# Other costs for TensorE's products and a longer table of places in a list scheduler: the same 5635 instructions in another order

## The chip, the cores and the metric

The kernel runs on one core of a Trainium2 chip. The metric is the device time of one execution in microseconds (us). Five engines work side by side, each through its own instructions in a fixed order: TensorE (PE, products and transposes; its weight loads are listed as PEld), VectorE (DVE), ScalarE (ACT), GpSimd (POOL) and SyncE (SP, which issues most transfers). An instruction also waits for semaphores that other engines raise.

## The reference

```python
def hybrid_parallel_heads_encoder(x, ...):          # x: 1 x 256 x 1024, fp32, two layers
    ...
    h = rms_norm(x, norm1_g) @ w_in                 # 1024 -> 2560: q, k, v of three groups
    a = neighbourhood_attention(...)                # 4 heads
    d = dilated_window_attention(...)               # 6 heads
    c = grouped_query_attention(...)                # 6 heads, 2 of k and v
    x = x + rms_norm of each group, joined @ w_out
    g, u = split(rms_norm(x, norm2_g) @ w_gate_up)  # 1024 -> 2 x 2816
    g = depthwise convolution of width 3 over g, + bias
    x = x + (silu(g) * u) @ w_down                  # 2816 -> 1024
```

## The kernel before

Every fp32 product is made as three products of two parts, `hi` (the value cut to the product format) and `lo` (what is left): hi*hi, lo*hi and hi*lo. So each weight chunk that lands in a `wp_raw` buffer is cast to `wp_hi` on ACT, and DVE subtracts the two into `wp_lo`. The sequence is two tiles of 128 tokens. A layer has an attention part (projections from `act_hT`, the normalised and transposed input; scores, softmax, transposes of the probabilities, products with the values; the output projection from `act_mixT`) and a feed-forward part in 11 steps of 256 columns, each with a gate (G), an up (U) and a down product. Products collect in PSUM tiles `psa_a` (four buffers) and `psw_w` (four buffers).

Nothing of this is issued as it is written. Each call only adds an operation to a list (class `Plan`); `order()` then plays through a list scheduler in which each operation has a cost from `cost()`, each handover between engines one from `HANDOVER`, and each buffer a time from which it is free. Of all operations that are ready it takes the one that can start earliest; where several can, the one with the lowest rank decides. The rank is the operation's number in the list plus a shift; `PLACES` adds to the rank of single operations, by their number. `emit()` (line 472) issues everything in that order, so every instruction of the trace carries that line. The order on each engine is fixed when the program is built; on the chip the engines only wait for each other.

Names that the prediction uses: `const_x` is the residual, and holds the result at the end; `act_s2k` is scratch; `act_z` and `act_sw` serve the rotary embedding; `act_nab` is the neighbourhood bias, which POOL copies out of `small_few`; `small_ms`, `small_rstd` and `small_rx` are statistics of the norms; `act_ch` and `act_cl` are the hi and lo part of one step's activation in the feed-forward part. The very last product tile of layer 2 is cut in two halves of 256 columns, so that its second half, `end`, has a PSUM tile of its own, a DVE instruction of 256 columns and an output transfer of 128 KB.

Of the kernel before, what the change touches and what calls it, by code (L numbers as in the profile page):

```python
# [224 lines left out]
def handover(a, b):  # L225
# [1 line left out]


PLACES = {
# [6 lines left out]
}  # L236


class Plan:
# [30 lines left out]
    def add(self, engine, method, args, kw):  # L270
# [14 lines left out]
        if method == "matmul" and not kw["start"]:  # L285
            ins.append(args[0])
        o.ns, o.lat, o.size, o.kind = cost(engine.name, method, args, kw, ins)
        func = args[2] if method == "activation" else None
        if func in (AF.Exp, AF.Gelu) and func != self.table:
# [185 lines left out]
def cost(engine, method, args, kw, ins):  # L475

    out = args[0]
    if method == "dma_start":
        w = out if isinstance(out, View) else args[1]
        small = min(out.shape[-1], args[1].shape[-1]) < 128  # L480
        spread = isinstance(args[1], bass.AP) and args[1].ap[0][0] == 0
        stored = isinstance(out, View) and out.tile.pool.dram
        size = 4 * math.prod(w.shape) * (2 if small or spread else 1.5 if stored else 1)
        return 620 if engine == "POOL" else 480, 0, size, None
    n = out.width()
    psum = any(v.tile.pool.psum for v in ins)
    if engine == "PE":
        if method == "transpose":
            return n / 2.25 + 2.5, 0, 0, "turn"
        n = args[2].width()  # L490
        ns = {512: 231.6, 384: 174.5, 256: 118.0}.get(n, n / 2.25 + 2.5)
        if args[1].dtype == mybir.dt.bfloat16:
            ns = 213.0
        return ns, 0, 0, "half" if args[1].shape[0] < P else "full"
    if engine == "ACT":
        extra = 88 * sum(isinstance(kw.get(k), View) for k in ("scale", "bias")) + 92 * ("accum_out" in kw)
        ns = 0.833 * n + (53 if psum else 95) + extra
        return ns, ns + (15 if "accum_out" in kw else 105), 0, None
    if engine == "DVE":
        if method in ("reduce_sum", "reduce_max"):  # L500
            n = args[1].width()
        ns = 1.04 * n + (126 if method == "scalar_tensor_tensor" else 68)
        return ns, ns + 82, 0, None
    if method == "memset":
        ns = 190 + 0.83 * n
    elif method == "tensor_copy":
        ns = 0.92 * n + 100
    elif kw.get("op") == ALU.pow:
        ns = 560 + 150 * n
    elif method == "tensor_scalar":  # L510
        ns = 350 + 3.8 * n
    else:
        ns = 830 if out.width() == S else 350 + 3.1 * n
    return ns, ns - 95, 0, None
# [1046 lines left out]
```

## Time and profile before

| | |
|---|---|
| time, median of 3 runs | 604.28 us (603.97 to 604.68) |
| the profiled execution's own time | 604.39 us |
| its span in the trace | 602.6 us |
| PE busy | 596.9 us |
| DVE, ACT, POOL busy | 484.9, 428.5, 81.0 us |

The span runs from the first instruction to the last; 1.8 us of the profiled execution's time lie around it. Where the engine that is busy nearly all the time stands still, the whole kernel gets longer; where another engine does, that costs nothing by itself.

### The profile page before, as it was taken

The numbers are of one execution on the slowest core, as the hardware profiler recorded it, in microseconds if no ns is written. First come the engines' busy times: TensorE is split into PE (matmuls) and PEld (weight loads), VectorE is DVE, ScalarE is ACT, GpSimd is POOL, SyncE is SP. The second block draws the span as 40 slices with busy tenths as digits, with TensorE's granted clock in tenths as the row PEclk, the third lists the DMA queues.
The fourth block names the chain that finished last, engine by engine and source line by source line (L and its number), as shares of the span: only waits on it lengthen the run. The fifth ranks groups of instructions, "written<-read, shape, count | busy, mean of one in ns | idle before, by whom it ended". The sixth has DMA issues, their size and how long they took to land.

```text
span 602.6 us, 9916 instructions
## 1 busy us (share of the span) xinstructions
PE 596.9 (99%) x3496; PEld 524.7 (87%) x3496; DVE 484.9 (80%) x995; ACT 428.5 (71%) x1065; POOL 81.0 (13%) x130
## 2 busy tenths in 40 slices
PE   8999999999999999999999999999999999999997
PEld 7999898888888888888899989888888888888886
DVE  4899988997788988888777898777977777777775
ACT  6889999686566767666688899676766556666661
POOL 2733030102400000000023213421000000000000
PEclk9999999999999999999999999999999999999999
DMA  8893313557588898999444726844465556555501
GB/s 281 294 329 114 106 36 108 196 188 238 174 243 292 274 358 310 327 308 298 155 143 159 258 71 245 281 177 140 140 210 202 171 188 210 173 179 208 194 16 70
DMA packets 85218, 121.44 MB, mean 202 GB/s; under 512 B 9881, under 2 KB 69881, under 8 KB 85169
## 3 DMA queue, kind: packets, MB, share of 16 engines
q1 hardware_dynamic: 82896, 112.17, 55.8%
q0 software_dynamic: 1728, 8.39, 4.1%
q8 instruction: 27, 0.44, 0.3%
q10 hardware_dynamic: 544, 0.26, 0.1%
q14 instruction: 23, 0.18, 0.1%
HBM read 110.93 MB, written 9.88 MB: 200 GB/s over the span
## 4 chain that ended last, share of the span: by engine, by line
PE 97%; ACT 1%; DVE 1%; POOL 0%; issue 0%; DVEq 0%; POOLq 0%
PE psw_w L472 53%; PE psa_a L472 44%; ACT act_s2k L472 0%; POOL small_rstd L472 0%; ACT act_z L472 0%; DVE act_z L472 0%; ACT act_hT L472 0%; DVE wp_lo L472 0%; DVE act_sw L472 0%; POOL small_ms L472 0%; DVE const_x L472 0%; DVE act_qo L472 0%; ACT wp_hi L472 0%; POOL const_warm L472 0%; DVEq L472 0%
## 5 line engine op out<-in xcount | busy, mean ns | idle before, releaser
L472 DVE TENSOR_TENSOR wp_lo<-wp_raw,wp_hi 128x512 fp32r<-128x512 f32 (+2 forms) x332 | 231.8, 733 | 57.1 <-ACT wp_hi L472 41.1
L472 ACT CAST wp_hi<-wp_raw 128x512 fp32r<-128x512 f32 (+2 forms) x332 | 203.0, 663 | 21.7 <-PE psw_w L472 10.1
L472 PE MATMUL psw_w<-act_hT,wp_hi 128*128 128x512 f32 x704 | 180.3, 393 | 0.0
L472 PEld LDWEIGHTS psw_w<-act_hT,wp_hi 128*128 128x128 f32 x704 | 127.3, 188 | 24.5 <-DVE act_hT L472 0.6
L472 PE MATMUL psa_a<-wp_hi,act_hT 128*128 128x384 f32 (+2 forms) x448 | 112.6, 331 | 0.7 <-ACT wp_hi L472 0.7
L472 PEld LDWEIGHTS psw_w<-act_hT,wp_lo 128*128 128x128 f32 x704 | 97.2, 188 | 7.1
L472 PE MATMUL psw_w<-act_hT,wp_lo 128*128 128x256 f32 x704 | 101.3, 280 | 0.0
L472 PEld LDWEIGHTS psa_a<-wp_hi,act_hT 128*128 128x128 f32 x448 | 78.2, 188 | 3.4 <-ACT wp_hi L472 0.9
L472 PE MATMUL psa_a<-wp_lo,act_hT 128*128 128x384 f32 (+2 forms) x224 | 74.2, 333 | 0.1
L472 ACT COPY act_s2k<-psw_w 128x256 f32<-128x256 f32 x88 | 32.3, 372 | 58.5 <-PE psw_w L472 58.1
L472 PE MATMUL psa_a<-wp_lo,act_ch 128*128 128x512 f32 (+1 forms) x176 | 68.2, 387 | 0.0
L472 PE MATMUL psa_a<-wp_hi,act_ch 128*128 128x512 f32 x176 | 68.1, 388 | 0.0
L472 PE MATMUL psa_a<-wp_hi,act_cl 128*128 128x512 f32 (+1 forms) x176 | 67.6, 388 | 0.0
L472 DVE TENSOR_TENSOR act_s2k<-psw_w,act_s2k 128x256 f32<-128x256 f32 x88 | 36.7, 422 | 12.2 <-ACT act_s2k L472 11.8
L472 PEld LDWEIGHTS psa_a<-wp_lo,act_hT 128*128 128x128 f32 x224 | 42.1, 188 | 2.3 <-DVE wp_lo L472 1.0
L472 PEld LDWEIGHTS psa_a<-wp_hi,act_cl 128*128 128x128 f32 x176 | 33.1, 188 | 6.8
L472 PEld LDWEIGHTS psa_a<-wp_hi,act_ch 128*128 128x128 f32 x176 | 33.0, 188 | 6.2
L472 PEld LDWEIGHTS psa_a<-wp_lo,act_ch 128*128 128x128 f32 x176 | 33.1, 188 | 6.0
L472 DVE SCALAR_TENSOR_TENSOR act_s2k<-act_s2k,act_cw,act_s2k 128x255 f32<-128x255 f32 x88 | 36.8, 478 | 1.4 <-ACT act_s2k L472 1.3
L472 ACT ACTIVATE act_s2k<-act_s2k 128x512 f32<-128x512 f32 x22 | 13.9, 632 | 30.2 <-DVE act_s2k L472 30.2
L472 ACT ACTIVATE act_s2k<-act_s2k,act_cw 128x256 f32<-128x256 f32 x44 | 24.1, 595 | 15.4 <-DVE act_s2k L472 15.4
L472 POOL TENSOR_TENSOR small_rstd<-small_ms,const_mh 128x6 f32<-128x6 f32 (+2 forms) x26 | 30.8, 1186 | 14.2 <-DVE small_ms L472 12.6
(132 smaller groups left out, 791.7 us busy)
## 6 DMA issues: line engine op xcount, KB each, us to landing
wp_raw<-in_w_gate_up_dram SPq DMA_DIRECT2D x44, 1024.0 KB, 5.0
wp_raw<-in_w_down_dram SPq DMA_DIRECT2D x22, 1024.0 KB, 7.3
wp_raw<-in_w_in_dram SPq DMA_DIRECT2D x14, 768.0 KB, 5.9
wp_raw<-in_w_in_dram SPq DMA_DIRECT2D x8, 1024.0 KB, 7.0
wp_raw<-in_w_out_dram SPq DMA_DIRECT2D x8, 768.0 KB, 7.8
dram_khi<-act_mixT_hi SPq DMA_DIRECT2D x4, 768.0 KB, 3.6
dram_klo<-act_mixT_lo SPq DMA_DIRECT2D x4, 768.0 KB, 8.4
wp_lo<-dram_klo POOLq DMA_DIRECT2D x4, 768.0 KB, 5.0
```

The source lines that it names most:

```text
L472: getattr(o.engine.real, o.method)(*map(real, o.args), **{k: real(v) for k, v in o.kw.items()})
```

## The change

Three numbers in `cost()` are new, the times that the scheduler counts for a product of 512, 384 and 256 columns, and the table `PLACES` goes from 50 to 126 entries. No operation is added, removed or altered: what changes is where each stands on its engine.

```diff
 PLACES = {
-    375: -35, 488: 15, 528: -53, 550: 173, 587: -78, 594: 125, 616: -286, 646: -9, 709: -79, 750: -226, 752: -396,
+    71: -45, 87: 313, 90: -10, 97: 334, 125: 1139, 202: 544, 261: 285, 305: 481, 340: 437, 347: 207, 356: 412,
...
         n = args[2].width()
-        ns = {512: 231.6, 384: 174.5, 256: 118.0}.get(n, n / 2.25 + 2.5)
+        ns = {512: 228.6, 384: 173.8, 256: 117.8}.get(n, n / 2.25 + 2.5)
```

The orders differ most in the two attention parts and little in the feed-forward parts. Three places follow. The number behind a name is the buffer's and the tile's; a tile's can differ between the two programs by a little.

First, ACT at the start, some 13 us in: `wp_hi1` is cast from the second weight buffer, and `act_s2k...small_ssx` are squares of the residual, which the norm's statistics need. Before:

```order
L472 ACTIVATE act_hT0_146<-psw_w3_166,const_gains0_122 128x256
L472 ACTIVATE act_hT0_146<-psw_w1_117,const_gains0_122 128x256 x2
L472 ACTIVATE act_s2k4_223,small_ssx0_163<-const_x0_79 128x512
L472 ACTIVATE act_hT0_146<-psw_w2_124,const_gains0_122 128x256 x2
L472 ACTIVATE act_s2k0_81,small_ssx0_163<-const_x0_79 128x512
L472 CAST wp_hi1_240<-wp_raw1_138 128x384 x4
L472 CAST wp_hi0_141<-wp_raw2_153 128x384 x4
```

and after the change:

```order
L479 ACTIVATE act_s2k3_202,small_ssx0_163<-const_x0_79 128x512
L479 ACTIVATE act_hT0_146<-psw_w1_117,const_gains0_122 128x256 x2
L479 ACTIVATE act_s2k4_221,small_ssx0_163<-const_x0_79 128x512
L479 ACTIVATE act_hT0_146<-psw_w2_124,const_gains0_122 128x256
L479 CAST wp_hi1_233<-wp_raw1_138 128x384 x3
L479 ACTIVATE act_hT0_146<-psw_w2_124,const_gains0_122 128x256
L479 CAST wp_hi1_233<-wp_raw1_138 128x384
L479 ACTIVATE act_s2k0_81,small_ssx0_163<-const_x0_79 128x512
L479 CAST wp_hi0_141<-wp_raw2_153 128x384 x4
```

The last square stood ahead of the four casts from `wp_raw1`; it now stands behind them, and three of the casts also go ahead of the last `act_hT`.

Second, PE in the first projections, some 25 us in: the products into `psa_a3` are the keys of the dilated group for the second token tile, those into `psa_a0` are its values for the first, from the weights `wp_hi0` and `wp_lo0`. Before:

```order
L472 MATMUL psa_a3_332<-wp_hi1_240,act_hT0_146 128x384 x2
L472 MATMUL psa_a3_332<-wp_lo1_248,act_hT0_146 128x384
L472 MATMUL psa_a3_332<-wp_hi1_240,act_hT0_146 128x384 x2
L472 MATMUL psa_a3_332<-wp_lo1_248,act_hT0_146 128x384
L472 MATMUL psa_a3_332<-wp_hi1_240,act_hT0_146 128x384
L472 MATMUL psa_a0_157<-wp_hi0_141,act_hT0_146 128x384
L472 MATMUL psa_a0_157<-wp_lo0_149,act_hT0_146 128x384
L472 MATMUL psa_a0_157<-wp_hi0_141,act_hT0_146 128x384 x2
L472 MATMUL psa_a0_157<-wp_lo0_149,act_hT0_146 128x384
L472 MATMUL psa_a0_157<-wp_hi0_141,act_hT0_146 128x384 x2
L472 MATMUL psa_a0_157<-wp_lo0_149,act_hT0_146 128x384
L472 MATMUL psa_a0_157<-wp_hi0_141,act_hT0_146 128x384
```

and after the change:

```order
L479 MATMUL psa_a3_331<-wp_lo1_240,act_hT0_146 128x384
L479 MATMUL psa_a3_331<-wp_hi1_233,act_hT0_146 128x384
L479 MATMUL psa_a0_157<-wp_hi0_141,act_hT0_146 128x384
L479 MATMUL psa_a0_157<-wp_lo0_149,act_hT0_146 128x384
L479 MATMUL psa_a0_157<-wp_hi0_141,act_hT0_146 128x384 x2
L479 MATMUL psa_a0_157<-wp_lo0_149,act_hT0_146 128x384
L479 MATMUL psa_a0_157<-wp_hi0_141,act_hT0_146 128x384 x2
L479 MATMUL psa_a0_157<-wp_lo0_149,act_hT0_146 128x384
...
L479 MATMUL psa_a3_331<-wp_hi1_233,act_hT0_146 128x384
L479 MATMUL psa_a3_331<-wp_lo1_240,act_hT0_146 128x384
L479 MATMUL psa_a3_331<-wp_hi1_233,act_hT0_146 128x384 x2
L479 MATMUL psa_a3_331<-wp_lo1_240,act_hT0_146 128x384
```

The last six products of the keys now come after the values' first tile and a part of their second, so the values' first product stands six products earlier on PE.

Third, PE at the very end: `psw_w1` (before: `psw_w0`) is the half tile `end`. Before:

```order
L472 MATMUL psw_w0_83<-wp_lo1_248,act_ch1_828 128x256
L472 MATMUL psw_w0_83<-wp_hi1_240,act_cl1_838 128x256
L472 MATMUL psa_a0_157<-wp_lo0_149,act_ch0_762 128x512
L472 MATMUL psa_a0_157<-wp_hi0_141,act_cl0_783 128x512
L472 MATMUL psa_a0_157<-wp_hi1_240,act_ch1_828 128x512
L472 MATMUL psa_a0_157<-wp_lo1_248,act_ch1_828 128x512
L472 MATMUL psa_a0_157<-wp_hi1_240,act_cl1_838 128x512
L472 MATMUL psa_a0_157<-wp_hi1_240,act_ch1_828 128x512
L472 MATMUL psa_a0_157<-wp_lo1_248,act_ch1_828 128x512
L472 MATMUL psa_a0_157<-wp_hi1_240,act_cl1_838 128x512
```

and after the change:

```order
L479 MATMUL psw_w1_117<-wp_hi0_141,act_cl0_783 128x256
L479 MATMUL psw_w1_117<-wp_hi0_141,act_ch0_762 128x256
L479 MATMUL psw_w1_117<-wp_lo0_149,act_ch0_762 128x256
L479 MATMUL psw_w1_117<-wp_hi0_141,act_cl0_783 128x256
L479 MATMUL psw_w1_117<-wp_hi1_233,act_ch1_833 128x256
L479 MATMUL psw_w1_117<-wp_lo1_240,act_ch1_833 128x256
L479 MATMUL psw_w1_117<-wp_hi1_233,act_cl1_842 128x256
L479 MATMUL psw_w1_117<-wp_hi1_233,act_ch1_833 128x256
L479 MATMUL psw_w1_117<-wp_lo1_240,act_ch1_833 128x256
L479 MATMUL psw_w1_117<-wp_hi1_233,act_cl1_842 128x256
```

Before, the last products were eight of 512 columns into a whole tile; now they are those of the half tile, 256 columns each. The same holds behind them: DVE's last instruction and the last output transfer are now those of the half tile.

## Rows read from the trace of the kernel before

**Rows 1.** The page: busy time of PE with its share and instructions; TensorE's granted clock.

```profile
PE 596.9 (99%) x3496; PEld 524.7 (87%) x3496; DVE 484.9 (80%) x995; ACT 428.5 (71%) x1065; POOL 81.0 (13%) x130
...
PEclk9999999999999999999999999999999999999999
```

**Rows 2.** Windows, the start: stretch, length, then busy time of each engine.

```profile
0.00:16.00 16.00, 14.34 (x79) 11.52 (x80) 7.70 (x18) 10.99 (x27) 4.42 (x14) 1.00 0.88 287
```

**Rows 3.** The chain that ended last, one feed-forward step: start, length, what.

```profile
438.30 11.12 PE psw_w L472 x64
449.42 5.45 PE psa_a L472 x24
```

**Rows 4.** Timeline at the start, ACT and PE: start, us, instruction, idle before.

```profile
12.98 0.64 ACT L472 ACTIVATE act_s2k<-const_x 128x512 f32<-128x512 f32 x1
...
13.59 0.93 ACT L472 CAST wp_hi<-wp_raw 128x384 fp32r<-128x384 f32 x2
...
14.16 0.62 PE L472 MATMUL psa_a<-wp_hi,act_hT 128*128 128x384 f32 x2 [0.67 <-ACT wp_hi L472]
```

**Rows 5.** Timeline 24 to 29 us, and one row at 33 us; POOL, DVE, PE.

```profile
24.11 2.16 POOL L472 COPY act_nab<-small_few 28x1984 f32<-28x1984 f32 x1
...
24.49 1.96 DVE L472 TENSOR_TENSOR act_sw<-act_z,small_sdq 128x48 f32<-128x48 f32 x2
26.37 0.55 DVE L472 TENSOR_TENSOR wp_lo<-wp_raw,wp_hi 128x384 fp32r<-128x384 f32 x1
...
27.31 0.55 DVE L472 TENSOR_TENSOR wp_lo<-wp_raw,wp_hi 128x384 fp32r<-128x384 f32 x1
...
27.70 0.33 PE L472 MATMUL psa_a<-wp_lo,act_hT 128*128 128x384 f32 x1
...
28.21 0.33 PE L472 MATMUL psa_a<-wp_lo,act_hT 128*128 128x384 f32 x1
...
32.98 0.68 DVE L472 TENSOR_TENSOR act_sw<-act_z,small_sdk 128x48 f32<-128x48 f32 x2
```

**Rows 6.** Timeline of PE at 34 us.

```profile
34.42 0.34 PE L472 MATMUL psa_a<-wp_hi,act_hT 128*128 128x384 f32 x1
34.84 0.44 PE L472 MATMUL psa_a<-wp_lo,act_hT 128*128 128x384 f32 x1
```

**Rows 7.** Timeline 94 to 97 us, DVE and PE: first score tile, transposes.

```profile
94.70 0.42 DVE L472 CUSTOM_DVE_ANT_0 act_s2k<-psw_w,act_nab 128x256 f32<-128x256 f32 x1 [0.26 <-PE psw_w L472]
...
96.08 0.69 DVE L472 TENSOR_TENSOR wp_lo<-wp_raw,wp_hi 128x512 fp32r<-128x512 f32 x1
...
95.87 0.60 PE L472 MATMUL psw_w<-const_ident,act_s2k 128*128 128x128 f32 x4
```

**Rows 8.** Timeline of PE where layer 1's attention ends.

```profile
119.39 0.39 PE L472 MATMUL psa_a<-wp_hi,act_mixT_lo 128*128 128x512 f32 x1
119.78 0.50 PE L472 MATMUL psw_w<-act_hT,wp_hi 128*128 128x512 f32 x1
120.11 0.28 PE L472 MATMUL psw_w<-act_hT,wp_lo 128*128 128x256 f32 x1
```

**Rows 9.** The end: timeline of DVE; windows (DMA share and GB/s last).

```profile
596.88 0.48 DVE L472 SCALAR_TENSOR_TENSOR const_x<-psw_w,small_rx,const_x 128x256 f32<-128x256 f32 x1
598.70 0.75 DVE L472 SCALAR_TENSOR_TENSOR const_x<-psa_a,small_rx,const_x 128x512 f32<-128x512 f32 x1 [1.34 <-PE psa_a L472]
...
598.15:598.75 0.60, 0.51 (x3) 0.09 (x1) 0.05 (x1) 0.00 (x0) 0.00 (x0) 1.00 0.64 219
600.30:601.13 0.83, 0.00 (x0) 0.00 (x0) 0.00 (x0) 0.00 (x0) 0.00 (x0) 1.00 0.84 316
```

**Rows 10.** Timeline 445 to 449 us, ACT and DVE: one step's activation.

```profile
447.11 0.62 ACT L472 CAST act_ch<-act_s2k 128x512 fp32r<-128x512 f32 x1
...
445.25 1.22 DVE L472 TENSOR_TENSOR wp_lo<-wp_raw,wp_hi 128x1024 fp32r<-128x1024 f32 x1 [0.20 <-ACT wp_hi L472]
...
447.76 0.69 DVE L472 TENSOR_TENSOR act_cl<-act_s2k,act_ch 128x512 fp32r<-128x512 f32 x1 [0.28 <-ACT act_ch L472]
```

17 rows, old and new, of the table PLACES are left out of this document.

## The prediction

> **What bounds the kernel now.** I read the page first, for which engine is busy nearly all the time. PE works 596.9 of the 602.6 us of the span, and every slice of TensorE's clock shows the highest digit [rows 1], so there is no stretch at a lower granted clock that another order could win back. So the 602.6 − 596.9 = 5.7 us in which PE isn't busy are many small pieces. The windows say where the biggest heap lies: in the first 16 us PE is busy 14.34, which leaves 1.66 [rows 2]. The chain that ended last, read over one feed-forward step, shows how little the middle holds: 64 gate and up products take 11.12 us and end at 449.42, exactly where the 24 down products begin for their 5.45 [rows 3]. The step repeats eleven times in each layer. Nothing waits between its two halves, so nothing can be won there, only lost. I then read the timeline at each place where the two orders differ on PE or on what PE waits for. 3496 products of the same sizes are issued before and after, and the three new numbers are only the scheduler's; no product gets shorter. Only PE's waits, and what lies ahead of its first and behind its last product, can change.
>
> **The start.** ACT runs a square of the residual at 12.98 for 0.64 us, and the four casts from `wp_raw1` follow it at 13.59; PE, idle for 0.67, goes on at 14.16 with the first of those casts done [rows 4]. After the change three casts stand ahead of the last `act_hT`, and the square behind all of them. The casts come earlier by at most 13.59 − 12.98 = 0.61. But the `act_hT` that they overtake is an operand of products also, so some of it comes back as a later `act_hT`; one cast of the pair's 0.93 is 0.46, and I take **−0.47**, between 0 and −0.61. Everything behind it on PE comes earlier by as much, and meets the next supplier sooner.
>
> **The values of the dilated group, 25 to 29 us.** Here the change costs something. POOL copies the neighbourhood bias from 24.11 for 2.16, so until 26.27. DVE begins two `act_sw` products at 24.49, and the pair needs 1.96; the same pair for the keys needs 0.68 at 32.98, when no copy runs [rows 5]. Only behind them, at 26.37, comes the subtraction that makes chunk 2 of the values' `wp_lo`, done at 26.37 + 0.55 = 26.92, and chunk 3 at 27.31 + 0.55 = 27.86. PE took chunk 2 at 27.70 and chunk 3 at 28.21 [rows 5]: slacks of 0.78 and 0.35. None of these DVE steps moves earlier by the change, as long as the copy holds them.
>
> After the change the values' first product stands six products of 384 columns earlier. In the long run such a product takes 0.17 (0.33 of a row overlaps its successor), so 6 × 0.174 = 1.04, plus the 0.47 won at the start: PE asks for the values' parts 1.51 earlier. Two products of the first tile that stood between are pushed ahead as well, worth about 0.2. At chunk 2 PE then waits 1.51 − 0.78 − 0.2 = 0.53. At chunk 3 DVE delivers 27.86 − 26.92 = 0.94 after chunk 2, while PE comes back for it 28.21 − 27.70 = 0.51 later: another 0.43. After a wait PE starts a product with a larger step than in a steady stream (0.33 instead of 0.23 where it resumes at 119.78 [rows 8]), 0.10 each time, so 0.2. The sum is **+1.2** (0.53 + 0.43 + 0.2). It is bounded below by 0, if DVE is not held; above by 1.7, if the 0.2 isn't there and the keys left for later don't find their place.
>
> The Trainium skill, "SBUF — State Buffer", section "Who interferes with whom", says that a DVE instruction with two inputs in SBUF contends with a GpSimd instruction that reads SBUF, and that whoever issues first holds the shared ports for the whole instruction while the other blocks. The trace agrees in the end times (26.27 of the copy, 26.37 for DVE's next step); by that rule the whole 1.2 would turn round if `act_sw` were issued ahead of the copy.
>
> **At 34 us** PE goes from 34.42 to 34.84 between two products where the cadence is 0.17 [rows 6]; 0.25 of it is a wait for a `wp_lo`. The subtraction stands further ahead in the new order, but what follows it is tight also. I take **−0.17**, between 0 and −0.25.
>
> **The attention parts.** These are the most reordered. In layer 1, PE's transposes begin at 95.87 in a PSUM tile that DVE's scalings of the scores into `act_s2k` release; the first of them starts at 94.70. A `wp_lo` subtraction of 0.69 at 96.08 stood behind those scalings and now stands ahead of four of them [rows 7]. I read a slack of some 0.4 at this place, so 0.69 − 0.4 = 0.29 could show; half of it lies under other ready products: **+0.14**, between 0 and +0.7. At the other places that differ I found small gains and small losses of 0.1 to 0.3 that about cancel, and count them as 0 ± 0.3. Where this attention ends PE goes 119.39 to 119.78 (0.39) and 119.78 to 120.11 (0.33), against 0.23 for a product of 512 columns [rows 8] (5.45 / 24 in the down products [rows 3]): 0.16 + 0.10. Both are waits for the hi and lo parts of the next input; DVE now makes these ahead of the residual's additions: **−0.26**, between 0 and −0.26.
>
> **The end.** PE's last product before is one of 512 columns. DVE adds its tile to the residual from 598.70 for 0.75, and the 256 KB go out with the DMA engines busy for 0.83 at 316 GB/s [rows 9]. After the change the last tile is the half tile, whose DVE instruction of 256 columns took 0.48 and whose 128 KB went out in a window of 0.60 at 219 GB/s [rows 9]. So the tail gets shorter by 0.75 − 0.48 = 0.27 and by 0.83 − 0.60 = 0.23 to 0.25 (I take 0.25: the window's borders are not sharp): **−0.52**. What could take it back is the whole tile's transfer, which now goes before; the ten products of 256 columns that the order's third place shows give it 10 × 0.12 = 1.2, more than its DVE instruction's 0.75.
>
> The Trainium skill, "DMA: Bandwidth & Descriptors", section "Anatomy of one DMA", gives a fixed cost and bytes at 436 GB/s; 128 KB less would be an estimated −0.30 by that page, where the rows give −0.25.
>
> **The feed-forward parts** count as nothing. Their cover is thin in one place: the activation of a step is cast from 447.11, done at 447.73 [rows 10], and used by the down products from 449.42 [rows 3], so what gets ahead of it is paid once 1.7 us are gone; its `act_cl` is done at 448.45. In the places that I followed, the order of casts, subtractions and products keeps those distances.
>
> **The sum** is −0.47 + 1.2 − 0.17 + 0.14 − 0.26 − 0.52 = −0.08. Against the profiled execution's own 604.39 that gives 604.31; the median of the runs is 0.11 lower than that execution, so **604.2 us**. About 0.2% (1.2 us) is what a measurement of this kernel can tell from no change, and the forecast lies well inside: the same.
>
> **The rivals.** *A: the wait at 25 us doesn't come.* POOL's copy and DVE's first `act_sw` start 0.38 us apart (24.11 and 24.49 [rows 5]), and ACT and DVE work ahead of them moves by 0.47. If `act_sw` comes before the copy, or the copy elsewhere, the pair costs 0.68, chunk 2 is there 1.28 earlier, and the +1.2 falls away: 604.2 − 1.2 = 603.0, faster by 0.2%. For it speaks the short distance; against it that the copy needs nothing that DVE makes and so keeps its time, while `act_sw` stands behind a `wp_lo` subtraction on DVE.
>
> *B: a feed-forward step gives way, and the kernel gets slower.* Near 448 us, in the second step of layer 2, the last three products of the step's up tile now stand behind most of the next step's gate, and its activation can only begin when they are done. Behind them the order has 13 products of 0.23 and 6 of 0.12 (half the columns) until the down product, 3.7 us; before, a whole gate of 5.5 lay there. The `act_cl` part is asked for six down products later, at 3.7 + 6 × 0.23 = 5.1. On DVE it now stands behind a `wp_lo` subtraction of 1.22, and on ACT the `act_ch` cast behind two further casts of 0.62 [rows 10]. Followed through the new order with the durations of before, where those lie beside each other, `act_ch` is there after 2.6 and `act_cl` after 4.3: slacks of 1.1 and 0.8. It decides when the subtraction and the two casts come one after the other with that way instead of beside it: 1.22 + 1.24 − 0.8 = 1.66, and 604.2 + 1.66 = 605.9, slower. With one cast beside it the wait is 1.0 and the time 605.2, still the same by the bound. Against it: the casts need only buffers that the gate's earlier products have freed by then.
>
> *C: the order hardly matters*, since at nearly every place PE has other products ready, and start and end don't move either because the engine behind them isn't the one I read: each term goes to the end nearest nothing, but the tail's −0.52 stays: about 603.8, the same too.
>
> **How the numbers follow.** The forecast has 0.55, C 0.15, A 0.2, B 0.1. The forecast's own range is 603.5 to 604.9: the ±0.3 of the attention parts, the 0.47 that the start can lose and the 0.5 by which the wait at 25 us may be longer, not all at once. Up to 602.9 the range takes A in, and up to 605.2 the half of B with one cast ahead; outside lies under 2 in 10. Faster by over 0.2% (below 603.07) is most of A and a little of the forecast's and of C's edge, 0.2; slower (above 605.5) is the half of B with both ahead and a little more, 0.08; the same has 0.72.
>
> **What would show it.** Right: no idle of 0.67 on PE near 14 us; two waits of PE for a `wp_lo` of DVE between 25 and 28 us, together 1 us or more, while POOL's copy and `act_sw` still end together; steps of 0.17 at 34 us and of 0.23 where layer 1's attention ends; as DVE's last row one of 0.48 with 256 columns, and a last transfer of 0.6; feed-forward steps still 11.12 and 5.45 back to back. Wrong: a pair of `act_sw` of 0.68 at 24 us (A); a wait of PE in front of the down products around 449 us (B); or a wait in an attention part that I counted as cancelled, above all one for a scaling or a transpose behind reordered DVE work.

## The result: slower by 0.4%, and the profile after

The changed kernel takes 606.48 us (median of 6, 606.29 to 607.18) where the one before took 604.18 in the same runs: a ratio of 1.0040, with a 95% interval of 1.0027 to 1.0053. The forecast was 604.2. The profiled execution took 606.86 with a span of 605.1, against 604.39 and 602.6 before.

Of the page, the busy times and the clock answer to [rows 1]:

```profile
PE 598.2 (99%) x3496; PEld 524.5 (87%) x3496; DVE 485.8 (80%) x995; ACT 427.4 (71%) x1065; POOL 85.6 (14%) x130
...
PEclk9999999999999999999999999999999999999999
```

The clock is the same. DVE and ACT do what they did. POOL, with 130 instructions as before, is busy 85.6 us instead of 81.0 [rows 1]: with the same work, that is a first hint. The view of waits lists for what PE stood still (us in total, times, longest); beside the 1.0 us for `const_warm` at the very start, which is there before and after, it has these:

```profile
PE psa_a L479 <- DVE wp_lo L479: 0.8, 1, 0.8
PE psa_a L479 <- ACT wp_hi L479: 0.7, 1, 0.7
PE psw_w L479 <- POOL small_rx L479: 0.3, 1, 0.3
PE psw_w L479 <- POOL act_sqm L479: 0.3, 1, 0.3
```

None of these four was there before; the wait of 0.7 for a `wp_hi` that [rows 4] shows at 14 us is gone, and this one of the same size is at 52 us. The timeline of PE shows where they lie; the first number is when the product started that had waited:

```profile
22.63 0.44 PE L479 MATMUL psa_a<-wp_lo,act_hT 128*128 128x384 f32 x1
...
27.37 0.44 PE L479 MATMUL psa_a<-wp_lo,act_hT 128*128 128x384 f32 x1 [0.81 <-DVE wp_lo L479]
27.65 0.51 PE L479 MATMUL psa_a<-wp_hi,act_hT 128*128 128x384 f32 x2
28.30 0.44 PE L479 MATMUL psa_a<-wp_lo,act_hT 128*128 128x384 f32 x1
...
52.29 0.74 PE L479 MATMUL psa_a<-wp_hi,act_hT 128*128 128x512 f32 x3 [0.67 <-ACT wp_hi L479]
...
113.81 0.33 PE L479 MATMUL psw_w<-const_ident,act_sqm 128*128 128x128 f32 x1 [0.25 <-POOL act_sqm L479]
...
127.51 0.43 PE L479 MATMUL psw_w<-const_ident,small_rx 128*128 128x128 f32 x2 [0.29 <-POOL small_rx L479]
```

Idle time begins where a product's row ends, but products overlap, so a place is priced by its steps from start to start, less the usual step. At 27 us three products start at 26.04, 26.22 and 27.37: the last step is 1.15 in place of 0.17, so 0.98. The steps that follow are 0.28 (the **restart**, the first step behind a wait, 0.11 too long), 0.48 from 27.82 to 28.30 (0.31) and a restart of 0.11 again: 1.50 in all. By the same reading 22 us costs 0.34, 51 us 0.94, 113 us 0.47 and 127 us 0.49. The five together are 3.74 us.

What the other engines did there is in the timelines of POOL and DVE:

```profile
24.50 2.16 POOL L479 COPY act_nab<-small_few 28x1984 f32<-28x1984 f32 x1
...
24.89 1.96 DVE L479 TENSOR_TENSOR act_sw<-act_z,small_sdq 128x48 f32<-128x48 f32 x2
...
46.32 1.36 POOL L479 TENSOR_SCALAR small_ms<-small_ss,small_he 128x6 f32<-128x6 f32 x1 [9.18 <-DVE wp_lo L479]
...
49.11 0.56 DVE L479 TENSOR_TENSOR act_z<-psa_a,small_rstd 128x384 f32<-128x384 f32 x1 [1.24 <-POOL small_rstd L479]
...
111.27 1.89 DVE L479 TENSOR_TENSOR wp_lo<-wp_raw,wp_hi 128x512 fp32r<-128x512 f32 x3
112.19 1.56 POOL L479 TENSOR_TENSOR act_sqm<-act_sqm,act_sqm 128x256 f32<-128x256 f32 x1 [2.95 <-ACT act_sqm L479]
...
125.34 1.28 DVE L479 TENSOR_TENSOR wp_lo<-wp_raw,wp_hi 128x512 fp32r<-128x512 f32 x2
125.39 1.29 POOL L479 TENSOR_SCALAR small_mex<-small_s1x 128x2 f32<-128x2 f32 x1
```

The same three POOL instructions in the kernel before, from its timeline:

```profile
44.92 0.56 POOL L472 TENSOR_SCALAR small_ms<-small_ss,small_he 128x6 f32<-128x6 f32 x1 [9.21 <-ACT act_s2k L472]
...
112.06 0.74 POOL L472 TENSOR_TENSOR act_sqm<-act_sqm,act_sqm 128x256 f32<-128x256 f32 x1 [5.17 <-ACT act_sqm L472]
...
122.91 0.19 POOL L472 TENSOR_SCALAR small_mex<-small_s1x 128x2 f32<-128x2 f32 x1
```

So `small_ms` takes 1.36 in place of 0.56 (which was a shorter meeting already, as one of the experiments shows), `act_sqm` 1.56 in place of 0.74 and `small_mex`, an operation on two numbers in each row, 1.29 in place of 0.19, each while DVE runs weight subtractions or a product with both inputs in SBUF. It is the meeting that was forecast at 25 us, in the other direction: there POOL's copy holds DVE, here DVE holds POOL. Four of the five new places (all but 22 us, where a weight chunk's cast and subtraction stand behind two others) are read as such meetings; the experiments take them apart. At 48 us the way is longest: POOL's `small_rstd` is late, DVE's `act_z` scaling waits for it 1.24, the next scaling of scores stands behind that on DVE, a softmax on ACT waits for the scaling, a weight cast stands behind the softmax, and PE waits for the cast at 51.34.

The gains came as well. The windows' row for the first 16 us answers to [rows 2]:

```profile
0.00:16.00 16.00, 14.98 (x83) 12.18 (x84) 7.96 (x19) 10.93 (x28) 3.25 (x13) 1.00 0.88 290
```

PE does 83 products there, not 79, and the 0.67 of idle time is gone. The end, from the timeline of PE and DVE, answers to [rows 9]:

```profile
601.29 0.28 PE L479 MATMUL psw_w<-wp_hi,act_cl 128*128 128x256 f32 x1
601.61 0.48 DVE L479 SCALAR_TENSOR_TENSOR const_x<-psw_w,small_rx,const_x 128x256 f32<-128x256 f32 x1 [0.45 <-PE psw_w L479]
```

The feed-forward part, from the chain that ended last, at the place of [rows 3]:

```profile
435.71 5.49 PE psa_a L479 x24
441.19 14.11 PE psw_w L479 x77
455.30 5.44 PE psa_a L479 x24
```

The products are grouped otherwise (77 in a row), but each piece begins where the last one ends.

### The profile page after: what moved, and what is told of

The parts are those of the page before. It is cut to its first block, busy times and chain, and to the rows that moved or that the text cites. A ratio compares the mean times of both kernels' runs of the same rounds, so it can differ in the third digit from the quotient of the medians.

```text
span 605.1 us, 9914 instructions
## 1 busy us (share of the span) xinstructions
PE 598.2 (99%) x3496; PEld 524.5 (87%) x3496; DVE 485.8 (80%) x995; ACT 427.4 (71%) x1065; POOL 85.6 (14%) x130
## 4 chain that ended last, share of the span: by engine, by line
PE 89%; ACT 3%; DVE 3%; DMA 2%; POOL 1%; issue 1%; SPq 0%; DVEq 0%; POOLq 0%; ACTq 0%
PE psw_w L479 50%; PE psa_a L479 39%; DMA wp_raw<-in_w_in_dram 2%; ACT wp_hi L479 1%; DVE wp_lo L479 1%; ACT act_s2k L479 1%; ACT act_hT L479 1%; SPq L479 0%; DVE act_sw L479 0%; POOL small_rstd L479 0%; DVE act_z L479 0%; POOL act_sqm L479 0%; POOL small_ms L479 0%; DVE act_nab L479 0%; POOL small_mex L479 0%
## 5 line engine op out<-in xcount | busy, mean ns | idle before, releaser
L479 PE MATMUL psa_a<-wp_hi,act_ch 128*128 128x512 f32 (+1 forms) x176 | 68.3, 388 | 0.0
L479 POOL TENSOR_TENSOR small_rstd<-small_ms,const_mh 128x6 f32<-128x6 f32 (+2 forms) x26 | 32.4, 1246 | 14.9 <-DVE small_ms L479 13.2
```

What stands on the lines that cost most here:

```text
L479: getattr(o.engine.real, o.method)(*map(real, o.args), **{k: real(v) for k, v in o.kw.items()})
```

## The experiments

The theory at this point: PE is fed late where an instruction of POOL meets one of DVE with two inputs in SBUF (**meetings**). The rivals: the new order asks so early that its suppliers are late anyhow, or what is removed at one place comes back at the next; and, of the two parts of the change, the new product times rather than the table carry the loss.

Most kernels move single operations after the scheduler is done, by this edit; the list holds the operation, the one beside which it goes, and 1 for behind or 0 for ahead:

```diff
-            for i in self.order():
+            done = self.order()
+            for i, j, behind in MOVES:
+                done.remove(i)
+                done.insert(done.index(j) + behind, i)
+            for i in done:
                 o = self.ops[i]
+                if i in ON_ACT:
+                    self.tc.nc.scalar.copy(*map(real, o.args))
+                    continue
```

**The two parts of the change.** Three product times alone, with the table of before:

```diff
-        ns = {512: 231.6, 384: 174.5, 256: 118.0}.get(n, n / 2.25 + 2.5)
+        ns = {512: 228.6, 384: 173.8, 256: 117.8}.get(n, n / 2.25 + 2.5)
```

> The kernel before with the three new product times alone and its own table of 50 places. First theory (the loss comes from POOL and DVE meeting at a few places, which the new table brought about): the product times alone move some instructions but bring no such meeting in front of PE, so 604.2 within 0.6. Rival (the scheduler's product times are what pulls products ahead of their suppliers everywhere): most of the 2.3 us of loss is here, 606 or more.

Measured: 611.19 us, ratio 1.0114 (1.0098 to 1.0129). Then the new table alone, with the old product times:

> The changed kernel with the three old product times and the new table of 126 places. First theory: the meetings at 25, 46 and 112 us come from the table, so the loss stays, 606 to 607. Rival (the places were made for the new product times and lose only with them, or the times carry the loss): 604.5 or less, or clearly over 607.5 if the table without its times is worse still.

Measured: 608.80 us, ratio 1.0078 (1.0061 to 1.0095). My forecast of the first was wrong by 7 us, that of the second fell to its rival (the table without its times is worse still), and either part alone is worse than both. So the loss is neither the table's nor the times'. I read it so, without a run that shows it: product times that differ by 0.2 to 1.3% give another sequence, in which the same shifts reach other neighbours. The first one's profiled execution is 6.0 us longer than that of the kernel before, and 4.9 of these lie where layer 1's attention ends: 3.2 in two waits in PE's timeline (1.10 and 2.14 by their steps), most of the rest in TensorE's clock. Below the timeline's rows stand two of the windows (stretch, length, PE's busy time; the granted clock is third from the end):

```profile
120.56 0.87 PE L472 MATMUL psw_w<-const_ident,const_x 128*128 128x128 f32 x6 [0.94 <-DVE const_x L472]
123.42 0.50 PE L472 MATMUL psw_w<-act_hT,wp_hi 128*128 128x512 f32 x1 [1.98 <-DVE act_hT L472]
```

```profile
121.00:123.40 2.40, 0.44 (x4) 0.20 (x2) 2.40 (x6) 2.35 (x7) 0.00 (x0) 1.00 0.17 68
124.20:127.70 3.50, 3.50 (x16) 3.18 (x15) 3.50 (x7) 3.45 (x12) 1.34 (x2) 0.52 0.35 102
```

DVE does four residual additions of 2.79 us in a row and three weight subtractions of 1.88 there, and the transposes and the next input wait behind them. PE worked 0.44 of the 2.40 us up to 123.4, and from 124.2 to 127.7 the granted clock was 0.52 in the mean, the lower level (1.2 GHz): transposes step by 0.21 there and by 0.11 before. In no other profiled execution here does the granted clock fall ahead of PE's last product. In the second kernel, the waits at 26 and 51 us of the changed kernel are there again, with others.

**The copy.** POOL's copy of the bias is issued on ACT, at a place where ACT stood idle for 2.81 us:

```diff
+MOVES = [(308, 202, 1)]
+ON_ACT = (308,)
```

> The changed kernel with one instruction elsewhere: POOL's copy of the neighbourhood bias (2.16 us at 24.5) is issued on ACT, some 21 us in, where ACT stands idle for 2.8 us; PE, DVE and POOL keep their order. First theory (DVE's rotary product is held by the copy, whoever stands in the queue): the pair of products takes 0.3 to 0.7 us in place of 1.96, PE's waits of 0.98 and 0.31 us between 26 and 28.3 us go, and with their restarts the kernel gets 1.3 to 1.5 us shorter: 605.0 to 605.2. Rival (the values' products stand so far ahead on PE that DVE's queue is late even when nothing holds it): a wait of 0.5 us or more stays there and the time is 605.8 to 606.3.

Measured: 604.72 us, ratio 1.0009 (1.0000 to 1.0019): 1.76 shorter than the changed kernel, a little more than forecast, and 0.54 above the kernel before. ACT and DVE in its timeline:

```profile
20.62 1.84 ACT L488 COPY act_nab<-small_few 28x1984 f32<-28x1984 f32 x1
...
24.57 0.34 DVE L490 TENSOR_TENSOR act_sw<-act_z,small_sdq 128x48 f32<-128x48 f32 x2
```

The pair of `act_sw` takes 0.34 in place of 1.96 with nothing else moved on DVE, and between 26 and 29 us PE's only longer step is one of 0.26 behind transposes, as in the kernel before. The rival is out at this place. The waits at 50, 111 and 125 us are still there (0.82, 0.39, 0.47), as they must be.

**The same in the kernel before**, where PE did not wait at 27 us:

```diff
+MOVES = [(308, 208, 1)]
+ON_ACT = (308,)
```

> The kernel before with only the bias copy on ACT, some 21 us in. First theory (the copy cost something only because the new order used up the slack behind it): the pair of rotary products takes 0.3 to 0.7 in place of 1.96, PE waited for nothing there and waits for nothing now, 604.0 to 604.6, no difference. Rival (the copy costs in every order): 603.4 or less.

Measured: 604.16 us, ratio 0.9995 (0.9984 to 1.0007). The pair takes 0.31 there, and the time stays within these 0.7 us. PE's wait at 34 us (0.24 [rows 6]) is not in this trace, so the copy may have cost that much before also; runs do not resolve it. The hold was there before the change; what the change took away at 27 us was the cover.

**The cover.** The changed kernel with the six products of the keys put back:

```diff
+MOVES = [(261, 319, 0), (262, 319, 0), (263, 319, 0), (264, 319, 0), (265, 319, 0), (266, 319, 0)]
```

> The changed kernel with PE's order of before at one place: the last six products of the dilated keys go ahead of the values' first product again; POOL's copy stays where it is. First theory (the copy holds DVE, and the six products were the cover of that): the pair of rotary products still takes 1.96, and PE's waits of 0.98 and 0.31 with their restarts shrink by 1.0, the length of the six products, to 0.5 in all; 605.3 to 605.6. Rival (what was postponed on PE only fills a later hole, so nothing is won): 606.2 to 606.6, with a new wait of PE between 29 and 36 us.

Measured: 606.03 us, ratio 1.0027 (1.0016 to 1.0038), between the two expectations. POOL, DVE and PE:

```profile
24.77 1.83 POOL L486 COPY act_nab<-small_few 28x1984 f32<-28x1984 f32 x1
...
24.65 2.01 DVE L486 TENSOR_TENSOR act_sw<-act_z,small_sdq 128x48 f32<-128x48 f32 x2
```

```profile
28.12 0.44 PE L486 MATMUL psa_a<-wp_lo,act_hT 128*128 128x384 f32 x1
...
33.07 0.45 PE L486 MATMUL psa_a<-wp_lo,act_hT 128*128 128x384 f32 x1 [0.63 <-DVE wp_lo L486]
```

The copy still holds DVE, although the first of the two products now starts ahead of it: it is the second, from 24.80, that stands until the copy is done. The waits there shrink from 1.50 to 0.36 (a step from 27.70 to 28.12 and its restart), by the length of the six products. But the rival is right too: at 33 us a wait of 0.79 with a restart of 0.11 appears, for the values' next weights, which the postponed products had covered. Moving them moves the hole.

**One DVE instruction away from one POOL instruction.** On top of the copy on ACT, the product of bias and mask goes away from the moment at which `small_ms` comes due:

```diff
+MOVES = [(308, 202, 1), (729, 529, 1)]
+ON_ACT = (308,)
```

> The changed kernel with the bias copy on ACT (604.72) and one more move on DVE alone: a product of the bias with its mask (two inputs in SBUF), which stands at the moment when POOL's small_ms comes due (46 us), goes behind the second score scaling. Neither POOL's order nor what is queued behind DVE's wait changes. First theory (POOL's small_ms is held by DVE's instruction): small_ms takes 0.3 to 0.6 in place of 1.36, the scaling that waits for POOL starts 0.8 to 1.1 earlier, PE's wait of 0.82 and its restart of 0.11 at 50 us shrink to 0.3 or less in all, 603.9 to 604.1. Rival (the wait is one of DVE's queue: whatever POOL does, the rotary scaling in front of the score scalings is late): small_ms gets short but PE's wait stays over 0.6, 604.6 to 604.9.

Measured: 604.63 us, ratio 1.0004 (0.9994 to 1.0015), so a tenth under the kernel with the copy alone (three tenths, each against the kernel before in its own runs), not 0.7: the time lies in the rival's range, PE's wait between the two expectations. Its rows say why:

```profile
44.36 0.27 POOL L490 TENSOR_SCALAR small_ms<-small_ss,small_he 128x6 f32<-128x6 f32 x1 [9.20 <-DVE wp_lo L490]
44.72 1.32 POOL L490 TENSOR_TENSOR small_rstd<-small_ms,const_mh 128x6 f32<-128x6 f32 x1
...
44.80 0.69 DVE L490 TENSOR_TENSOR wp_lo<-wp_raw,wp_hi 128x512 fp32r<-128x512 f32 x1 [0.52 <-ACT wp_hi L490]
```

```profile
48.76 0.51 ACT L490 ACTIVATE act_s2k<-act_s2k,small_nm 128x256 f32<-128x256 f32 x1 [0.64 <-DVE small_nm L490]
49.27 0.60 ACT L490 CAST wp_hi<-wp_raw 128x512 fp32r<-128x512 f32 x1
```

The hold is shown: without DVE's instruction beside it, `small_ms` takes 0.27, not 1.36, in the same order on POOL. But I had put the product, 0.76 long, ahead of the third score scaling, so the softmax for which the cast waits came late by that, and PE's wait shrank only from 0.82 to 0.41.

**All meetings apart.** The copy on ACT, and small moves at 20, 48, 112 and 125 us:

```diff
+MOVES = [(308, 202, 1), (482, 529, 1), (1260, 1199, 1), (1360, 1408, 1), (1384, 1360, 1),
+         (1454, 1360, 1), (202, 206, 0), (203, 207, 0)]
+ON_ACT = (308,)
```

> The changed kernel with the copy on ACT and four small moves: one rotary scaling on DVE, which waits for POOL, behind the next score scaling (48 us); one weight subtraction behind a scaling that reads PSUM (112 us); two weight subtractions behind another such scaling (125 us); and one weight chunk's cast and subtraction ahead of two others (20 us). First theory: PE's waits at 22 us (0.34), 26 to 28 (1.50), 51 (0.94), 113 (0.47) and 127 us (0.49) go, together 3.7; 606.5 - 3.7 = 602.8, and with something given back later 602.6 to 603.4, under the kernel before. Rival (the waits come from PE being fed earlier than its suppliers can follow, and move on to the next place when one is removed): 604.5 or more, with new waits of PE within 10 us behind each removed one.

Measured: 604.31 us, ratio 1.0000 (0.9990 to 1.0009). POOL and PE:

```profile
109.88 0.96 POOL L490 TENSOR_TENSOR act_sqm<-act_sqm,act_sqm 128x256 f32<-128x256 f32 x1 [2.95 <-ACT act_sqm L490]
...
122.61 0.19 POOL L490 TENSOR_SCALAR small_mex<-small_s1x 128x2 f32<-128x2 f32 x1
```

```profile
125.66 0.73 PE L490 MATMUL psw_w<-act_hT,wp_hi 128*128 128x512 f32 x2 [0.62 <-DVE act_hT L490]
```

The POOL instructions are down to 0.96 and 0.19 (before the change 0.74 and 0.19), and PE's waits for them are gone; so is that at 22 us, and at 50 us 0.27 is left of 0.94. The time lies between the two expectations. But a wait of 0.78 is new at 125 us, made by my own move: the two subtractions stood between the two scalings of the second tile. Put behind both, and with the mask product moved also:

```diff
+MOVES = [(308, 202, 1), (482, 529, 1), (1260, 1199, 1), (1360, 1410, 1), (1384, 1360, 1),
+         (1454, 1360, 1), (202, 206, 0), (203, 207, 0), (729, 536, 1)]
```

> The changed kernel with the copy on ACT, the mask product behind the second score scaling, and the moves of the kernel with the meetings apart, but with the two weight subtractions at 125 us behind both scalings of the second tile and not between them, where they cost 0.78 in front of PE and 0.11 at its restart. First theory: those 0.89 come back, and up to 0.3 at 50 us: 604.31 - 0.89 - 0.2 = 603.2, within 0.4; against the kernel before faster by 0.1 to 0.2%. Rival (each wait that is taken away comes back further on): 604.0 or more.

Measured: 603.96 us, ratio 0.9996 (0.9987 to 1.0006): 0.35 shorter (0.56, each against the kernel before in its own runs), not 1.1. PE now waits 0.36 at 53 us (for a score scaling behind the mask product) and 0.29 at 124 us (for the subtraction that came too late; 0.10 more at the restart). Each was a DVE instruction put in front of something else, so the last kernel only chose other neighbours for these two:

```diff
+MOVES = [(308, 202, 1), (482, 529, 1), (1260, 1199, 1), (1360, 1400, 0), (1384, 1410, 1),
+         (202, 206, 0), (203, 207, 0), (729, 592, 1)]
```

> The mended kernel with the two places put right at which its moves made new waits of PE: the mask product goes 7 us further back (0.36 at 53 us), and of the two weight subtractions at 122 us one goes ahead of the first pair of scalings and one behind the second (0.29 and 0.10 at 124 us). First theory: these 0.75 come back, 603.96 - 0.75 = 603.2, within 0.4, the first of these kernels clearly under the one before. Rival (DVE is so full there that what is moved makes the next thing late): 603.8 or more.

Measured: 603.49 us, ratio 0.9986 (0.9975 to 0.9998) against 604.41 in its own runs, within the forecast: the first of these kernels whose interval lies under 1, by 0.15%. No wait of PE from the table above is left. From the changed kernel to this one the profiled span goes from 605.1 to 601.2, by 3.9, and the median from 606.48 to 603.49, by 3.0; the five new places were worth 3.74. The upper end of that interval is close to 1, and the profiled execution, 602.98, is near the lower end of its runs (602.90 to 604.89): its PE is 0.41 ahead by the 65th product of 384 columns (20.43 in place of 20.84), where none of the moves had taken effect. Without this the span is 3.5 shorter, against 3.74.

**Only the two gains.** The kernel before with the start and the end of the changed one:

```diff
+MOVES = [(125, 99, 1), (126, 125, 1), (127, 126, 1), (128, 127, 1), (129, 128, 1), (308, 208, 1),
+         (5569, 5607, 0), (5570, 5607, 0), ...  (5576, 5607, 0), (5625, 5631, 0), (5626, 5625, 1)]
+ON_ACT = (308,)
```

> The kernel before with only the two edits that were forecast and seen as gains, the start (the last square of the residual behind the four casts) and the end (the half tile's products, its addition and its transfer last), and the bias copy on ACT so that the start's gain is not lost at 25 us. By the two terms as the changed kernel's trace shows them, 0.49 and 0.52: 604.18 - 1.0 = 603.2, within 0.4. Rival (the start's gain is lost again before the scores, as PE then waits for the same late weights): 603.6 to 603.9, the end's gain alone.

Measured: 603.89 us, ratio 0.9998 (0.9987 to 1.0009), not told from the kernel before. At the start, PE's wait for the cast is down to 0.10, but it waits 0.62 for the `wp_lo` behind it. DVE's row:

```profile
13.76 1.96 DVE L483 TENSOR_TENSOR wp_lo<-wp_raw,wp_hi 128x384 fp32r<-128x384 f32 x4
```

The casts end earlier, but DVE's first subtraction still stands behind scalings of `act_hT` and a copy. In the changed kernel DVE begins the subtractions at 13.05, since there the casts go ahead of an `act_hT` as well: so I read the order on two engines as the gain; no run gives the kernel before both. At the end the last addition begins 0.34 behind PE and takes 0.48, but the span ends 3.46 after it, where it is 2.99 in the changed kernel and 3.15 before; the transfers of the last three tiles are issued closer to each other here. That they hold each other up is argued from this, not shown. So neither gain came whole: from the last product's start to the span's end it is 4.28 in place of 4.33, and at the start some 0.1. The time lies in the rival's range, but not by the rival's account, which left the end its 0.52.

## Why the prediction was wrong, by its own steps

**The step that failed** is "at the other places that differ I found small gains and small losses of 0.1 to 0.3 that about cancel, and count them as 0 ± 0.3". Those places hold new waits of 0.94, 0.47 and 0.49, and one more in the projections, 0.34 at 22 us; against them stands the 0.21 that went at 73 us. Three of the four are the mechanism of the 25-us term, which I had applied only where the trace of before showed it at work (DVE held by POOL). At the other places I kept the POOL durations of before (0.56, 0.74, 0.19) without saying so, though the new order put other DVE instructions beside them. The size of the failure shows in the kernel with only the copy on ACT: without the 25-us place the change costs 0.54, where all terms but the +1.2 add up to −1.28. Slower had a chance of 0.08, nearly all by way of a feed-forward step, which did not give way. In an order that moves DVE's instructions, the duration of a POOL instruction is no constant.

**25 us:** forecast +1.2 within 0 to 1.7, measured +1.50; the mechanism was right, as the copy on ACT and the keys show, and so rival A (the wait does not come) was out. The wait for chunk 2 was 0.98 where I had 0.53: POOL's copy began at 24.50 in place of 24.11 [rows 5], and DVE's subtractions came later by as much. The argument that the copy keeps its time was wrong: POOL's `small_rstd` ahead of it, at 22.14, took 1.61 in place of 1.32, beside a subtraction of DVE.

**Start:** forecast −0.47; the 0.67 is gone, a step that is 0.20 too long came instead of one of 0.14, and PE starts its 65th product of 384 columns at 20.84 in place of 21.45, so −0.6. Right, though the run with only the square moved shows that I named half of its cause.

**34 us:** forecast −0.17, measured −0.35 with the restart (no longer step but one behind transposes); mis-sized, as I had left out the restart that I counted at 25 us. **95 us:** forecast +0.14, no wait seen. **End of layer 1's attention:** forecast −0.26; the waits of [rows 8] and one like the second further on are gone, together 0.38; one of 0.09 is new.

**End:** forecast −0.52, and from the last product's start to the span's end it is 3.80 after, 4.33 before: −0.53. The parts were not as forecast: 0.27 for DVE as expected, but 0.16 for the transfer and what follows (2.99 in place of 3.15), not 0.25 or the estimated 0.30, and 0.11 because a product of 256 columns hands over sooner (0.32 in place of 0.43), which I had not counted. That the total is right to 0.01 is luck.

**Feed-forward:** forecast 0, right; rival B's place at 448 us shows pieces that touch. Rival C was out. The sum with what was measured: new waits 3.74, less 0.6 at the start, 0.35, 0.38, 0.21 and 0.53, gives +1.7; the profiled executions differ by 2.47. The rest, some 0.8, lies in pieces of 0.2 and less, half of it in layer 2's attention, which I did not take apart by runs.

**The clock** was read too widely. The page's digits show no lower level, but PE's products of 256 columns ahead of the first projections (`const_warm`) step by 0.21 until 6.4 us in both kernels. The orders there are alike, so no term changes. But in the profiled execution of the last kernel made from the changed one, the same products in the same order step by 0.11 from 5.1 us on, half of it, as between the two clock levels: some tenths of difference between two single executions can come from this.

The Trainium skill, "SBUF — State Buffer", section "Who interferes with whom", has the rule that was needed: a DVE instruction with two inputs in SBUF contends with a GpSimd instruction that reads SBUF, and the order of issue decides which of them blocks. The trace agrees on both directions (`act_sw` 1.96 against 0.34, `small_ms` 1.36 against 0.27). But not every instruction pair that overlaps blocks: in the kernel with the mask product moved, POOL's `small_rstd` runs 1.32 from 44.72 and DVE's subtraction beside it, from 44.80, takes its usual 0.69.

## What to carry to other kernels

A scheduler's order is as good as its durations. At 512 columns the new product time, 228.6 ns, is nearer to PE's step than the old one, 231.6 (5.45 / 24 us of [rows 3] is 227), and the order got worse all the same, since PE's new waits are for other engines. Where two engines hold each other, a duration depends on the neighbour: before trusting a new order, list every short POOL instruction that PE or DVE later waits for, and look at which DVE instructions now stand beside it. A shift table belongs to the costs with which it was made; change one alone and the order is that of neither. On an engine that is 80% busy, a move easily cures one wait and makes the next: four of the eight edited orders here did so, and each was seen only in the trace.

## What was not expected of the hardware

A POOL instruction that meets DVE can stand for more than one instruction. `small_mex` came at 125.39, when DVE was in the first of two subtractions, and ended at 126.68, just behind the end of both (125.34 + 1.28 = 126.62); `act_sqm` came at 112.19 in the second of three and ended at 113.75, its usual 0.74 after 113.01, where the third was near its end (113.16).

It is no rule, though. Elsewhere POOL gets its turn between two DVE instructions that follow each other without a gap. At 25 us the copy began at 24.50, inside a subtraction of DVE, and the `act_sw` behind that, at 24.89, stood until the copy was done. And at 150 us POOL went on inside a run of DVE. From the changed kernel's timelines, DVE at 24 us, then POOL and DVE at 150 us:

```profile
24.34 0.62 DVE L479 TENSOR_TENSOR wp_lo<-wp_raw,wp_hi 128x384 fp32r<-128x384 f32 x1
...
149.89 0.91 POOL L479 TENSOR_TENSOR act_cck<-const_rot,const_gk 128x128 f32<-128x128 f32 x1
150.75 1.58 POOL L479 TENSOR_TENSOR act_sck<-const_rot,const_gk 128x32 f32<-128x32 f32 x3
...
149.12 2.89 DVE L479 TENSOR_TENSOR wp_lo<-wp_raw,wp_hi 128x512 fp32r<-128x512 f32 x4 [1.27 <-ACT wp_hi L479]
```

DVE's four subtractions run to 152.01, yet `act_cck` is done at 150.80. So the price of a meeting lies between what is left of one DVE instruction and what is left of the run; what decides between them is not shown here.
